# A hybrid decoder layer: the gated up projection as seven half-size products per pair of column tiles, with weight sums made by DMAs

## The chip, the cores and the metric

One core of a Trainium2 chip runs the whole layer. The time is device microseconds (us) of one execution; lower is better. The five engines are TensorE (PE, its weight loads shown apart as PEld), VectorE (DVE), ScalarE (ACT), GpSimd (POOL) and SyncE (SP, which only issues DMAs here).

## The reference, cut to what matters

The input x is 1024 tokens by 1024 channels in float32. The layer is a mixer (dilated attention heads beside mLSTM heads) and a gated ConvFFN, each with a residual; only the second is touched by the change.

```
def _conv_ffn(h, w_ffn_up, ffn_conv_w, ffn_conv_b, w_ffn_down):
    u = _causal_dwconv(h @ w_ffn_up, ffn_conv_w, ffn_conv_b)   # 1024 -> 2 x 2816, three taps over tokens
    gate, val = jnp.split(u, 2, axis=-1)
    return (jax.nn.silu(gate) * val) @ w_ffn_down               # 2816 -> 1024
...
h = h + _hybrid_mixer(_rmsnorm(h, mixer_norm_w[layer]), ...)
h = h + _conv_ffn(_rmsnorm(h, ffn_norm_w[layer]), ...)
return _rmsnorm(h, final_norm_w)
```

## The kernel before, in words

Every large product is computed from float32 operands split in two parts of a narrower format, a high part (a rounded copy) and a low part (the operand minus that copy). `mm3` issues three matmuls for one product: high by high, high by low, low by high. All matmuls of the up and down projections have a 128x128 stationary and a 512 wide moving operand and accumulate in one of eight PSUM banks (`bank`).

The kernel text is a planner. Each piece of work is a generator (a "lane") with a priority; `Clock` keeps an estimate of when each engine, tile and page is free, and `Lanes.run` takes the next lane that can go on. So the order of every engine's instructions is fixed when the program is built, and each engine runs its own list in order. SBUF tiles come from 48 pages of 128x1040 float32 (`page`, `free`); a lane waits until enough pages are free (`keep`). All plain loads and stores go through SP's queue in one order (`dma`, `store`).

The stages in order of time: input projection with mLSTM and attention (to about 530 us), output projection with the second norm (`output`, `h2`, to about 590 us), up projection (`upward`, to about 1070 us), down projection (`downward`, to the end).

- `h2` takes a finished residual tile `h` (128 tokens), normalises it into `xn2`, has PE transpose it in two groups of four, and writes the transposed tile as a high part `x2h` (ACT) and a low part `x2l` (DVE). The residual tiles `h` stay in SBUF to the end.
- `ufeed` loads the 44 column tiles of the up weights, 512 KB each, and splits them (`w..h`, `w..l`).
- `upward` walks the 44 column tiles (a gate tile, then the value tile of the same pair; 22 pairs). Each tile takes two token halves, and each half is 8 x 3 = 24 matmuls into one bank. `conv` then reads the bank: ACT writes the last tap into `ua`, DVE adds the other two taps, two small `edge` operations carry two tokens over the border of the halves; silu on the gate tile, and one product of both tiles. Gated tiles 0 to 7 stay in SBUF (`KEEP`), the other 14 are stored to DRAM (`gp`) and loaded again (`g`) for the down projection.
- `downward` already uses seven half-size products in place of eight (`seq`, `add_d`), with operands `A` (gated tiles) and `B` (down weights, loaded as `br`). Sums of quarters of the down weights are made in DRAM early on by `sums`: 4 copies issued by ACT and 7 adding DMAs issued by POOL, 2816 KB each, into `tsum`.

Two operations that can run on DVE or POOL are given to whichever the planner expects to finish first (`two`).

Of the kernel before, what the change touches and what calls it, by code (L numbers as in the profile page):

```python
# [15 lines left out]
S = 1024  # L16
D = 1024
# [206 lines left out]
def tile_hybrid_layer(ctx, tc, xT, x, w_t, w_v, w_g, w_o, w_up, w_dq, params, fnw, c_id, c_att, c_sel,  # L224
# [13 lines left out]
    tsum = {p: dram.tile([DFF // 2, 512], F32, name=f"tsum{p}") for p in (4, 5, 6, 7)}  # L238
    ctx.enter_context(tc.manual_schedule())
# [530 lines left out]
    def sums():  # L770

        quarter = lambda a, b: w_dq[a, b].rearrange("(r c) n -> r (c n)", c=4)
        into = {p: t.rearrange("(r c) n -> r (c n)", c=4) for p, t in tsum.items()}
        t = 100
        for p, b in ((5, (0, 0)), (6, (1, 1)), (7, (0, 1)), (4, (1, 0))):
            yield need(cond=lambda: clk.eng.get("pe", 0.0) > t)
            nc.scalar.dma_start(into[p], quarter(*b))
            t += 25
        for p, b in ((5, (0, 1)), (6, (0, 0)), (7, (1, 1)), (4, (1, 1)), (6, (0, 1)), (4, (0, 0)), (4, (0, 1))):
            yield need(cond=lambda: clk.eng.get("pe", 0.0) > t)  # L780
            nc.gpsimd.dma_start(into[p], quarter(*b), accum_op=OP.add, max_dma_last_dim=8192)
# [317 lines left out]
    ufeed = Feed([[w_up[c]] for c in range(2 * NK)], 2, 4, wait=lambda: "x2" in flags)  # L1099
    ufeed.start()  # L1100
# [17 lines left out]
    x2h, x2l = [], []  # L1118
# [13 lines left out]
    def output():  # L1132
# [52 lines left out]
    def h2(i, po):  # L1185
# [6 lines left out]
        for g in range(2):  # L1192
            yield need(xn_, bk=1)
            p = bank("ph2")
            for f in range(4):
                pe.transpose(p[:, f * 128:(f + 1) * 128], xn_[:, (g * 4 + f) * 128:(g * 4 + f + 1) * 128], ident)
            yield need(p)
            for f in range(4):
                ft = g * 4 + f
                wc = pr[:, P_FN + ft:P_FN + ft + 1]  # L1200
                ps_ = p[:, f * 128:(f + 1) * 128]
                act.activation(x2h[ft][:, ts], ps_, AF.Copy, scale=wc)
            yield need(x2h[g * 4 + 3])
# [11 lines left out]
        half_ready[i] = max(clk.ready(x2l[7]), clk.ready(x2l[3]))  # L1215
# [7 lines left out]
    KEEP = 8  # L1223
    LA = 5
    gate, gpage, gparked = {}, {}, set()
    gp = [dram.tile([128, 1024], F32, name=f"gp{k}") for k in range(NK)]

    def conv(c, ps):
        ch = (c // 2) + (c % 2) * NK
        cw = lambda j: pr[:, P_FW + ch * 3 + j:P_FW + ch * 3 + j + 1]  # L1230
        edge = small.tile([128, 2], F32, name="edge", bufs=4)
        for hf in range(2):
            yield need(pg=0 if hf else 1, cond=lambda: fin_ready(ps, hf))
            if hf == 0:
                a = page("ua")
            p = ps[hf]
            ah = a[:, H[hf]]
            act.activation(ah, p, AF.Identity, scale=cw(2), bias=pr[:, P_FB + ch:P_FB + ch + 1])
            yield need(a)
            for j in (1, 0):  # L1240
                sh = 2 - j
                dve.scalar_tensor_tensor(ah[:, sh:], p[:, :512 - sh], cw(j), ah[:, sh:], op0=OP.mult, op1=OP.add)
            if hf == 0:
                dve.tensor_scalar(edge, p[:, 510:512], cw(0), None, op0=OP.mult)
                dve.scalar_tensor_tensor(edge[:, 0:1], p[:, 511:512], cw(1), edge[:, 0:1], op0=OP.mult, op1=OP.add)
            else:
                dve.tensor_add(ah[:, 0:2], ah[:, 0:2], edge)
            freebank(p)
        yield need(a)
        if c % 2 == 0:  # L1250
            act.activation(a[:, :S], a[:, :S], AF.Silu)
            gate[c // 2] = a
        else:
            k = c // 2
            yield need(cond=lambda: k in gate)
            g = gate.pop(k)
            yield need(g)
            dve.tensor_mul(a[:, :S], a[:, :S], g[:, :S])
            free(g)
            if k < KEEP:  # L1260
                gpage[k] = a
            else:
                yield need(a)
                store(gp[k], a[:, :S])
                free(a)
                gparked.add(k)
# [56 lines left out]
    ADD, SUB = OP.add, OP.subtract  # L1323
# [7 lines left out]
    L, U = slice(0, 512), slice(512, 1024)  # L1331
# [9 lines left out]
    def split(t, src):  # L1341

        copy(t[:, L], src)
        yield need(t[:, L])
        two(t[:, U], src, f32(t[:, L]), OP.subtract)
# [75 lines left out]
    def add_d(j, p, to, done):  # L1421
        yield need(p)
        for th, hf, op in to:
            i = 4 * th + j
            dve.tensor_tensor(hp[i][:, H[hf]], hp[i][:, H[hf]], p, op=op)
# [5 lines left out]
        yield need(hp[i], pg=2)  # L1431
# [5 lines left out]
        act.activation(junk[:, h_], hp[i][:, h_], AF.Square, accum_out=(st2, st3)[hf][:, i:i + 1])  # L1437
        dve.tensor_mul(outs[i][:, h_], hp[i][:, h_], fins[0][:, h_])
# [18 lines left out]
    lanes.add(reload_gates(), 1)  # L1457
    lanes.add(b_load(), 1.1)
# [87 lines left out]
```

## Time and profile before

| | |
|---|---|
| median of 3 runs | 1291.52 us (1290.19 to 1293.23) |
| profiled execution | 1292.97 us |
| its span, first to last instruction | 1291.1 us |
| PE busy | 1277.5 us, 99% |
| DVE, ACT, POOL busy | 772.0, 502.8, 275.5 us |
| DMA traffic | 136.42 MB |

The page has busy time by engine, the span in 40 slices, the chain of work that ended last, and the costliest groups. All recorded instructions carry line 153, a helper that records every operation, so groups are told apart by their tiles (out <- in) and shapes. A matmul's row gives a duration longer than its share of the engine, since matmuls overlap; the pace is read from how many start in a stretch.

### The profile page before, as it was taken

What the parts mean: (1) busy time and instruction counts of PE and PEld (TensorE: products, weight loads), DVE (VectorE), ACT (ScalarE), POOL (GpSimd) and SP (SyncE); (2) the same over time, 40 slices, a digit from 0 to 9 for tenths busy, and PEclk for the clock granted to TensorE, in tenths of its full rate; (3) what the DMA queues carried; (4) which work ended last, traced back from release to release, by engine and by line L of the source; (5) the groups of instructions that cost most, each with busy time, mean ns of one, the idle gap of its engine ahead of it and who ended that gap; (6) DMA issues with size and microseconds to landing.
All of it is one profiled execution on the core that took longest, in us unless ns stands there. A gap on an engine that the chain in (4) does not pass through costs nothing.

```text
span 1291.1 us, 17082 instructions
## 1 busy us (share of the span) xinstructions
PE 1277.5 (99%) x6630; PEld 1079.7 (84%) x6630; DVE 772.0 (60%) x1511; ACT 502.8 (39%) x932; POOL 275.5 (21%) x162
## 2 busy tenths in 40 slices
PE   9999999999999989999999999999999999999997
PEld 6899898988998978888888888888888888888886
DVE  6726766678768786465343444434443556877865
ACT  4454354457656665153211121121212224243553
POOL 4420113022122022100222222222122110425002
PEclk9999999999999999999999999999999999999999
DMA  9404546651717552012111111313121217432324
GB/s 334 156 1 139 196 170 158 172 139 41 155 35 199 126 198 99 1 33 82 49 49 34 49 33 50 98 49 98 49 90 57 74 58 280 153 96 85 106 90 147
DMA packets 41001, 136.42 MB, mean 106 GB/s; under 512 B 4404, under 2 KB 5940, under 8 KB 38200
## 3 DMA queue, kind: packets, MB, share of 16 engines
q1 hardware_dynamic: 38024, 103.61, 23.5%
q0 software_dynamic: 2576, 20.19, 7.9%
q10 hardware_dynamic: 320, 11.53, 2.6%
q8 instruction: 52, 0.85, 0.3%
q14 instruction: 29, 0.24, 0.1%
HBM read 119.58 MB, written 47.45 MB: 129 GB/s over the span
## 4 chain that ended last, share of the span: by engine, by line
PE 95%; DVE 2%; ACT 1%; SPq 1%; issue 0%; DMA 0%; POOL 0%; POOLq 0%; DVEq 0%
PE bank L153 95%; DVE gu L153 1%; SPq L290 1%; DVE rows L153 0%; DMA xr<-in_xT_dram 0%; DVE q L153 0%; ACT L153 0%; DVE lf L153 0%; DVE ge L153 0%; ACT P L153 0%; ACT w1h L153 0%; ACT PT L153 0%; POOL w0l L153 0%; DVE gt L153 0%; DVE kS L153 0%
## 5 line engine op out<-in xcount | busy, mean ns | idle before, releaser
L153 DVE SCALAR_TENSOR_TENSOR ua<-bank,pr,ua 128x511 f32<-128x511 f32 (+1 forms) x176 | 131.9, 749 | 267.4 <-ACT ua L153 264.3
L153 PE MATMUL bank<-B,A 128*128 128x512 f32 x924 | 213.7, 393 | 0.0
L153 PEld LDWEIGHTS bank<-B,A 128*128 128x128 f32 x924 | 173.6, 188 | 40.0
L153 ACT ACTIVATE ua<-bank,pr 128x512 f32<-128x512 f32 x88 | 68.6, 779 | 341.0 <-PE bank L153 340.4
L153 DVE TENSOR_TENSOR h<-h,bank 128x512 f32<-128x512 f32 x88 | 56.9, 683 | 50.2 <-PE bank L153 50.2
L153 DVE CUSTOM_DVE_ANT_0 P<-bank,matt 128x512 f32<-128x512 f32 (+3 forms) x96 | 50.5, 551 | 14.9 <-PE bank L153 14.7
L153 ACT ACTIVATE P<-P,nmx 128x128 f32<-128x128 f32 (+3 forms) x64 | 49.4, 774 | 17.8 <-DVE nmx L153 16.8
L153 DVE TENSOR_TENSOR B<-br,B 128x512 fp32r<-128x512 f32 x67 | 49.7, 743 | 8.1 <-ACT B L153 7.9
L153 DVE TENSOR_TENSOR PT<-bank,PT 128x512 fp32r<-128x512 f32 (+1 forms) x80 | 47.7, 629 | 6.4 <-ACT PT L153 6.0
L153 PEld LDWEIGHTS bank<-PT,av 128*128 128x128 f32 x320 | 44.9, 192 | 3.8 <-DVE PT L153 1.5
L153 PE MATMUL bank<-PT,av 128*128 128x256 f32 (+1 forms) x320 | 46.9, 281 | 1.0 <-DVE PT L153 1.0
L153 ACT ACTIVATE B<-br 128x512 fp32r<-128x512 f32 x68 | 42.0, 620 | 6.1 <-DMA br<-in_w_dq_dram 4.1
L153 PE MATMUL bank<-kS,q 128*128 128x512 f32 (+3 forms) x192 | 41.9, 351 | 2.2 <-DVE OT L153 2.2
L153 ACT ACTIVATE PT<-bank 128x512 fp32r<-128x512 f32 (+1 forms) x72 | 37.4, 550 | 16.5 <-PE bank L153 15.0
L153 ACT ACTIVATE A<-g 128x512 fp32r<-128x512 f32 x45 | 28.0, 625 | 35.9 <-PE bank L153 15.9
L153 PE MATMUL bank<-ident,P 128*128 128x128 f32 x288 | 39.4, 274 | 0.2 <-ACT P L153 0.2
L153 ACT ACTIVATE A<-ua 128x512 fp32r<-128x512 f32 x31 | 19.4, 629 | 50.0 <-DVE ua L153 37.4
L153 ACT ACTIVATE ua<-ua 128x1024 f32<-128x1024 f32 x22 | 23.3, 1060 | 39.4 <-DVE ua L153 39.4
L153 PEld LDWEIGHTS bank<-kS,q 128*128 128x128 f32 x192 | 31.7, 192 | 6.1 <-issue 2.6
L153 POOL TENSOR_TENSOR rs<-st,half 128x1 f32<-128x1 f32 x16 | 12.1, 761 | 109.5 <-DVE st L153 109.5
L153 PEld LDWEIGHTS bank<-ident,P 128*128 128x128 f32 x288 | 32.4, 141 | 3.0 <-ACT P L153 1.2
L153 DVE SCALAR_TENSOR_TENSOR mqk<-mz,pr,mqk 128x1023 f32<-128x1023 f32 (+2 forms) x24 | 34.4, 1459 | 0.0
(674 smaller groups left out, 3579.6 us busy)
## 6 DMA issues: line engine op xcount, KB each, us to landing
wr<-in_w_up_dram SPq DMA_DIRECT2D x44, 512.0 KB, 3.8
tsum<-in_w_dq_dram POOLq DMA_DIRECT2D x7, 2816.0 KB, 17.5
tsum<-in_w_dq_dram ACTq DMA_DIRECT2D x4, 2816.0 KB, 11.4
br<-tsum SPq DMA_DIRECT2D x44, 256.0 KB, 2.7
br<-in_w_dq_dram SPq DMA_DIRECT2D x33, 256.0 KB, 2.7
gp<-ua SPq DMA_DIRECT2D x14, 512.0 KB, 2.9
g<-gp SPq DMA_DIRECT2D x14, 512.0 KB, 7.2
wr<-in_w_t_dram SPq DMA_DIRECT2D x13, 512.0 KB, 4.8
```

The lines of the kernel that those rows point to most:

```text
L153: r = f(*a, **k)
L290: nc.sync.dma_start(dst, src)
```

## The change

The up projection of a pair is now treated as a 2 by 2 block product: rows are the gate and the value tile, the inner dimension is cut in two halves of 512 channels, the columns are the two token halves. Seven products of half the inner length (4 x 3 = 12 matmuls each, numbered 1 to 7) take the place of eight.

- Input side: `h2` writes the transposed tiles unsplit into `x2f` (ACT alone). New lanes `x_block` make seven operand blocks `xb1` to `xb7` of four pages each (high part in the lower, low part in the upper half of a page): blocks 1, 2, 3 are parts of x2f, blocks 6, 5, 7, 4 are differences made in place by `two` (with four pages `xt`), each then split.
- Weight side: `usum` holds four summed quarters of the up weights in DRAM, made by `sums` with ACT copies and adding POOL DMAs of 5632 KB each, one after the other (5 from weights; 6 from 5; 3 from 6; 7 from weights). The sums for the down weights are now made the same way (4 copies, 4 adding DMAs) and later. `u_load` loads 256 KB per product into halves of a page `ur`; `u_side` splits it into `W`.
- Order of products: for the first four pairs 1 and 2 of each pair, then 3 of each, then 6, 5, 7, 4 pair by pair; for the other 18 pairs 1, 2, 6, 5, 3, 7, 4.
- `u_evac` combines the products with the sums in `ut`, partly in the bank itself, and `conv_half` does the taps for one half.
- All 22 gated tiles are stored and reloaded; the residual tiles are stored to `hpark` after `h2` and reloaded as `hq` in the down stage.

The core of the diff:

```
-            act.activation(x2h[ft][:, ts], ps_, AF.Copy, scale=wc)
-            dve.scalar_tensor_tensor(x2l[ft][:, ts], ps_, wc, f32(x2h[ft][:, ts]), op0=OP.mult, op1=OP.subtract)
+            act.activation(x2f[ft][:, ts], p[:, f * 128:(f + 1) * 128], AF.Copy, scale=wc)
+        store(hpark[i], hp[i][:, :S])
+        free(hp[i])
...
+    lanes.add(sums(70, 55, uq, usum, ((5, (1, 0), 0), (5, (1, 1), 1), (6, 5, 0), (6, (0, 0), 1), (3, 6, 0),
+                                      (3, (0, 1), 1), (7, (1, 0), 0), (7, (0, 0), 1))), 0.5)
+    lanes.add(sums(530, 45, dq, tsum, ((5, (0, 0), 0), (5, (0, 1), 1), (6, 5, 0), (6, (1, 1), 1), (4, 6, 0),
+                                       (4, (1, 0), 1), (7, (0, 1), 0), (7, (1, 1), 1))), 0.6)
...
+    usteps = [(c, p) for c in range(NP) for p in (1, 2)] + [(c, 3) for c in range(NP)]
+    usteps += [(c, p) for c in range(NP) for p in (6, 5, 7, 4)]
+    usteps += [(c, p) for c in range(NP, NK) for p in (1, 2, 6, 5, 3, 7, 4)]
...
-                    for k in range(8):
-                        mm3(p, wh[:, ks], wl[:, ks], x2h[k][:, sl], x2l[k][:, sl], k == 0, k == 7)
+            for f in range(4):
+                mm3(b, w[:, fs], w[:, fl], x_[:, L], x_[:, U], f == 0, f == 3)
+            lanes.add(u_evac(c, p, b), 3)
...
+        if p == 2:
+            dve.tensor_tensor(b, b, t[:, L], op=ADD)
+            yield from conv_half(c, 0, 0, b)
+        elif p == 6:
+            dve.tensor_tensor(t[:, L], t[:, L], b, op=SUB)
...
+        elif p == 7:
+            dve.tensor_tensor(t[:, L], t[:, L], b, op=ADD)
+            b = q5.pop(c)
+            dve.tensor_tensor(b, b, t[:, L], op=SUB)
+            yield from conv_half(c, 1, 1, b)
+        else:
+            dve.tensor_tensor(b, b, t[:, L], op=SUB)
+            yield from conv_half(c, 1, 0, b)
...
+    def reload_h():
+        for i in (0, 4, 1, 5, 2, 6, 3, 7):
+            yield need(pg=1, keep=8, cond=lambda: "up" in flags and used[0] > 2)
+            dma(hq[i][:, :S], hpark[i])
```

PE, where the up stage begins, before: x2h and x2l are the moving tiles of one channel block, w0h and w0l the split weights, and the transposes are of token tiles 6 and 7.

```order
L153 MATMUL bank3_86<-x2h0_5190,w0h_5216 128x512
L153 MATMUL bank3_86<-x2l0_5191,w0h_5216 128x512
L153 MATMUL bank3_86<-x2h0_5190,w0l_5217 128x512
L153 MATMUL bank6_89<-ident_92,xn2_5605 128x128 x4
L153 MATMUL bank3_86<-x2h1_5192,w0h_5216 128x512
L153 MATMUL bank3_86<-x2l1_5193,w0h_5216 128x512
```

So the three matmuls of one channel block follow each other, eight blocks to a bank.

PE, the same place now: product 1 of the first pair, with the transposes of tiles 5 and 6 inside it, and the first matmuls of product 2.

```order
L153 MATMUL bank1_96<-xb1_5465,W_5219 128x512 x3
L153 MATMUL bank2_97<-ident_104,xn2_5589 128x128 x4
L153 MATMUL bank3_98<-ident_104,xn2_5589 128x128 x4
L153 MATMUL bank6_101<-ident_104,xn2_5591 128x128 x4
L153 MATMUL bank4_99<-ident_104,xn2_5591 128x128 x4
L153 MATMUL bank1_96<-xb1_5468,W_5219 128x512 x3
L153 MATMUL bank1_96<-xb1_5470,W_5219 128x512 x3
L153 MATMUL bank1_96<-xb1_5472,W_5219 128x512 x3
L153 MATMUL bank0_95<-xb2_5474,W_5222 128x512 x3
```

A bank is now complete after 12 matmuls instead of 24, and three tiles' transposes stand inside the up stage instead of two.

DVE, from the last normed tile `xn2` on, before: the split of one weight tile, the taps of the first bank, and the low parts of the tile's transposes.

```order
L153 TENSOR_SCALAR xn2_5669<-h7_4998,rs2_109 128x1024
L153 CAST w3h_5679<-wr3_5613 128x1024
L153 TENSOR_TENSOR w3l_5680<-wr3_5613,w3h_5679 128x1024
L153 SCALAR_TENSOR_TENSOR ua_5677<-bank3_86,pr_91,ua_5677 128x511
L153 SCALAR_TENSOR_TENSOR ua_5677<-bank3_86,pr_91,ua_5677 128x510
L153 TENSOR_SCALAR edge_5622<-bank3_86,pr_91 128x2
L153 SCALAR_TENSOR_TENSOR edge_5622<-bank3_86,pr_91,edge_5622 128x1
L153 SCALAR_TENSOR_TENSOR x2l0_5191<-bank7_90,pr_91,x2h0_5190 128x128
```

Seven more x2l follow, and with them the operands of the whole up stage were complete.

DVE, the end of what stands there now, ahead of the first product 7: the last of blocks 7 and 4, a combination of product 6, and the low part of that product's weights (W_5979).

```order
L153 TENSOR_TENSOR W_5939<-ur_5793,W_5939 128x512
L153 TENSOR_TENSOR xb4_5909<-x2f5_5204,xb4_5909 128x512
L153 TENSOR_TENSOR xb7_5927<-xt_5731,xb7_5927 128x512
L153 TENSOR_TENSOR x2f6_5205<-x2f6_5205,xt_5731 128x512
L153 TENSOR_TENSOR xb7_5929<-xt_5732,xb7_5929 128x512
L153 TENSOR_TENSOR x2f7_5206<-x2f7_5206,xt_5732 128x512
L153 TENSOR_TENSOR ut_5645<-ut_5645,bank1_96 128x512
L153 TENSOR_TENSOR xb4_5946<-x2f6_5205,xb4_5946 128x512
L153 TENSOR_TENSOR W_5979<-ur_5976,W_5979 128x512
```

From the last `xn2` to W_5979 there are now 62 DVE instructions: 38 additions or subtractions of two SBUF tiles, 3 casts, 5 that take a bank, 8 taps and 8 edge operations.

ACT, in the input projection, before: a plain copy of a quarter of the down weights.

```order
L153 ACTIVATE va2_1577<-bank0_83,rn_101 128x128
L153 ACTIVATE va3_1579<-bank0_83,rn_101 128x128
L777 DMA tsum4_77<-in_w_dq_dram 64x11264
L153 ACT_TABLE_LOAD
L153 ACTIVATE mqk_1504<-mqk_1504 128x1024
```

Its source is an input, so ACT had nothing to wait for.

ACT, a few instructions further on in the same place now: a copy out of a sum that POOL's adding DMA has to have finished.

```order
L153 ACTIVATE mqk_1515<-mqk_1515 128x1024
L153 ACTIVATE va2_1588<-bank4_99,rn_113 128x128
L153 ACTIVATE va3_1590<-bank4_99,rn_113 128x128
L783 DMA usum6_83<-usum5_82 128x11264
L153 ACTIVATE va2_1588<-bank6_101,rn_113 128x128
```

Here ACT waits until that adding DMA has landed, with everything behind it on its queue. The adding DMA stands on POOL behind the split of w5 (`w5l`) and ahead of that of w6; two such waits of ACT lie in the input projection (usum6 from usum5, usum3 from usum6). Apart from the DMA issues that moved, the order of the engines before the second norm is as it was.

## Rows read from the trace of the kernel before

**Rows 1.** The page: busy time by engine, and the chain that ended last.
```profile
PE 1277.5 (99%) x6630; PEld 1079.7 (84%) x6630; DVE 772.0 (60%) x1511; ACT 502.8 (39%) x932; POOL 275.5 (21%) x162
PE 95%; DVE 2%; ACT 1%; SPq 1%; issue 0%; DMA 0%; POOL 0%; POOLq 0%; DVEq 0%
```
**Rows 2.** Stretches: us, busy PE (count) PEld DVE ACT POOL, PEclk, DMA share, GB/s.
```profile
579.80:1065.00 485.20, 485.20 (x2107) 393.86 (x2106) 215.06 (x397) 102.27 (x135) 96.84 (x41) 1.00 0.19 62
700.00:800.00 100.00, 100.00 (x434) 81.17 (x433) 41.09 (x77) 19.33 (x23) 21.66 (x9) 1.00 0.16 48
```
**Rows 3.** DVE, whole span, groups by shape: operation, count, busy us, mean ns, idle before.
```profile
L153 DVE SCALAR_TENSOR_TENSOR ua<-bank,pr,ua 128x511 f32<-128x511 f32 x88 | 66.0, 749 | 264.3 <-ACT ua L153 264.3
...
L153 DVE TENSOR_TENSOR h<-h,bank 128x512 f32<-128x512 f32 x88 | 56.9, 683 | 50.2 <-PE bank L153 50.2
...
L153 DVE TENSOR_TENSOR ua<-ua 128x1024 f32<-128x1024 f32 x22 | 27.0, 1225 | 0.7
...
L153 DVE TENSOR_TENSOR A<-g,A 128x512 fp32r<-128x512 f32 x37 | 25.5, 691 | 9.6 <-ACT A L153 9.5
...
L153 DVE SCALAR_TENSOR_TENSOR edge<-bank,pr,edge 128x1 f32<-128x1 f32 x44 | 9.6, 219 | 1.6
```
**Rows 4.** ACT, whole span, groups by shape.
```profile
L153 ACT ACTIVATE ua<-bank,pr 128x512 f32<-128x512 f32 x88 | 68.6, 779 | 341.0 <-PE bank L153 340.4 <-DVE B L153 0.6
L153 ACT ACTIVATE B<-br 128x512 fp32r<-128x512 f32 x68 | 42.0, 620 | 6.1 <-DMA br<-in_w_dq_dram 4.1 <-DVE B L153 1.3 <-POOL B L153 0.6
...
L153 ACT ACTIVATE ua<-ua 128x1024 f32<-128x1024 f32 x22 | 23.3, 1060 | 39.4 <-DVE ua L153 39.4
```
**Rows 5.** POOL from 1065 us on, groups by shape.
```profile
L153 POOL TENSOR_TENSOR B<-br,B 128x512 fp32r<-128x512 f32 x10 | 13.5, 1347 | 0.0
```
**Rows 6.** Timeline of PE in the second norm: start, us, engine, operation.
```profile
561.43 0.60 PE L153 MATMUL bank<-ident,xn 128*128 128x128 f32 x4
561.78 0.48 PE L153 MATMUL bank<-w2h,yh 128*128 128x512 f32 x1
```
**Rows 7.** Timeline of ACT, same stage.
```profile
581.32 1.14 ACT L153 ACTIVATE x2h<-bank,pr 128x128 fp32r<-128x128 f32 x4 [2.26 <-PE bank L153]
```
**Rows 8.** Timeline of DVE and POOL in the down projection.
```profile
1093.60 1.52 POOL L153 TENSOR_TENSOR ua<-ua,g 128x512 f32<-128x512 f32 x1 [50.80 <-DMA g<-gp]
1093.88 1.80 DVE L153 TENSOR_TENSOR ua<-ua,g 128x512 f32<-128x512 f32 x1
...
1099.11 9.66 DVE L153 TENSOR_TENSOR h<-h,bank 128x512 f32<-128x512 f32 x16 [1.38 <-PE bank L153]
...
1102.15 1.30 POOL L153 TENSOR_TENSOR A<-ua,A 128x512 fp32r<-128x512 f32 x1 [0.74 <-ACT A L153]
```
**Rows 9.** Stretches of 5 us around the one longer gap of PE, columns as in Rows 2.
```profile
455.00:460.00 5.00, 4.46 (x26) 3.46 (x25) 4.86 (x17) 3.55 (x7) 3.48 (x2) 1.00 1.02 416
...
465.00:470.00 5.00, 2.80 (x15) 2.02 (x14) 4.94 (x7) 3.00 (x5) 0.21 (x2) 1.00 0.05 20
470.00:475.00 5.00, 5.00 (x27) 4.76 (x26) 3.50 (x15) 1.70 (x7) 0.00 (x0) 0.66 0.38 108
```
**Rows 10.** DMA issues of the page: KB each, median us to landing.
```profile
wr<-in_w_up_dram SPq DMA_DIRECT2D x44, 512.0 KB, 3.8
...
tsum<-in_w_dq_dram ACTq DMA_DIRECT2D x4, 2816.0 KB, 11.4
...
g<-gp SPq DMA_DIRECT2D x14, 512.0 KB, 7.2
```
**Rows 11.** POOL's adding DMAs of 2816 KB (the line that issues them).
```profile
L781 POOL DMA_DIRECT2D tsum<-in_w_dq_dram x7: 920/982/1135, 197.6 to 415.7; - x7
...
DMA to landing us min/median/max: 17.1/17.5/20.5
```
**Rows 12.** Timeline of POOL in the input projection.
```profile
127.50 2.78 POOL L153 TENSOR_TENSOR w5l<-wr,w5h 128x1024 fp32r<-128x1024 f32 x1 [46.74 <-DVE ge L153]
```
**Rows 13.** Timeline of ACT in the input projection.
```profile
184.89 0.61 ACT L153 ACTIVATE va<-bank,rn 128x128 f32<-128x128 f32 x2
```

More of the change, by code (lines that the diff above doesn't have):

```diff
@@ L238, in tile_hybrid_layer @@
     tsum = {p: dram.tile([DFF // 2, 512], F32, name=f"tsum{p}") for p in (4, 5, 6, 7)}
+    usum = {p: dram.tile([DFF, 512], F32, name=f"usum{p}") for p in (3, 5, 6, 7)}
+    hpark = [dram.tile([128, 1024], F32, name=f"hpark{i}") for i in range(8)]
     ctx.enter_context(tc.manual_schedule())
@@ L1222, in tile_hybrid_layer @@
     NH = NK // 2
-    KEEP = 8
     LA = 5
+    LU = 5
+    NP = 4
     gate, gpage, gparked = {}, {}, set()
     gp = [dram.tile([128, 1024], F32, name=f"gp{k}") for k in range(NK)]
-    def conv(c, ps):
-        ch = (c // 2) + (c % 2) * NK
-        cw = lambda j: pr[:, P_FW + ch * 3 + j:P_FW + ch * 3 + j + 1]
[L1231 to L1245, printed above, removed]
-            else:
[L1247 to L1252, printed above, removed]
-        else:
[L1254 to L1266, printed above, removed]
@@ new lines, in tile_hybrid_layer, with two, split @@
+    L, U = slice(0, 512), slice(512, 1024)
+    ADD, SUB = OP.add, OP.subtract
+    def two(out_, a, b, op):
+        end = {}
+        for n in ("dve", "pool"):
+            c = clk.cost(n, "tensor_tensor", [out_], [a, b], {})
+            end[n] = clk.start(n, c, [out_], [a, b]) + c
+        (pool if end["pool"] + 0.3 < end["dve"] else dve).tensor_tensor(out_, a, b, op=op)
+    def split(t, src):
+        copy(t[:, L], src)
+        yield need(t[:, L])
+        two(t[:, U], src, f32(t[:, L]), SUB)
@@ new lines, in blocks_ready, with x_block @@
+    def blocks_ready(hf):
+        r = [half_ready.get(i, INF) for i in range(4 * hf, 4 * hf + 4)]
+        return max(r) if max(r) < INF else False
+    xb = {}
+    def x_block(p, f, src, wait, sums=(), done=()):
+        yield need(pg=1, keep=2, cond=wait)
+        t = page(f"xb{p}", F32R)
+        for s_ in sums:
+            two(*[s_[0](), s_[1](), s_[2]()], SUB)
+        yield need(src())
+        yield from split(t, src())
+        xb.setdefault(p, {})[f] = t
+        for d in done:
+            free(d())
@@ new lines, in u_side, with conv_half @@
+    def u_side():
+        for n in range(len(usteps)):
+            yield need(cond=lambda: n in uraw and n < uused[0] + LU)
+            r = uraw.pop(n)
+            src = r[:, (L, U)[n % 2]]
+            yield need(src, pg=1, keep=1 if xdone() else 2)
+            t = page("W", F32R)
+            yield from split(t, src)
+            if n % 2:
+                free(r)
+            Ub[n] = t
+    lanes.add(u_load(), 1.3)
+    lanes.add(u_side(), 2.5)
+    ut, ua, q5, edges = {}, {}, {}, {}
+    def conv_half(c, isv, hf, p, held=True):
+        ch = c + isv * NK
+        cw = lambda j: pr[:, P_FW + ch * 3 + j:P_FW + ch * 3 + j + 1]
+        if hf == 0:
+            yield need(pg=1)
+            ua[c, isv] = page("ua")
+            edges[c, isv] = small.tile([128, 2], F32, name="edge", bufs=8)
+        else:
+            yield need(cond=lambda: (c, isv, 0) in flags)
+        a, edge = ua[c, isv], edges[c, isv]
+        yield need(p)
+        ah = a[:, H[hf]]
+        act.activation(ah, p, AF.Identity, scale=cw(2), bias=pr[:, P_FB + ch:P_FB + ch + 1])
+        yield need(a)
+        for j in (1, 0):
+            sh = 2 - j
+            dve.scalar_tensor_tensor(ah[:, sh:], p[:, :512 - sh], cw(j), ah[:, sh:], op0=OP.mult, op1=OP.add)
+        if hf == 0:
+            dve.tensor_scalar(edge, p[:, 510:512], cw(0), None, op0=OP.mult)
+            dve.scalar_tensor_tensor(edge[:, 0:1], p[:, 511:512], cw(1), edge[:, 0:1], op0=OP.mult, op1=OP.add)
+        else:
+            dve.tensor_add(ah[:, 0:2], ah[:, 0:2], edge)
+        if held:
+            freebank(p)
+        flags.add((c, isv, hf))
+        if hf == 0:
+            return
+        del ua[c, isv], edges[c, isv]
+        yield need(a)
+        if not isv:
+            act.activation(a[:, :S], a[:, :S], AF.Silu)
+            gate[c] = a
+            return
+        yield need(cond=lambda: c in gate)
+        g = gate.pop(c)
+        yield need(g)
+        dve.tensor_mul(a[:, :S], a[:, :S], g[:, :S])
+        free(g)
+        yield need(a)
+        store(gp[c], a[:, :S])
+        free(a)
+        gparked.add(c)
@@ L1330, in tile_hybrid_layer @@
     used = [0]
-    L, U = slice(0, 512), slice(512, 1024)
-    def two(out_, a, b, op):
-        end = {}
-        for n in ("dve", "pool"):
-            c = clk.cost(n, "tensor_tensor", [out_], [a, b], {})
-            end[n] = clk.start(n, c, [out_], [a, b]) + c
-        (pool if end["pool"] + 0.3 < end["dve"] else dve).tensor_tensor(out_, a, b, op=op)
[L1341 to L1345, printed above, removed]
     def reload_gates():
-        for k in range(KEEP, NK):
-            yield need(pg=1, keep=6 if "up" in flags else 10, cond=lambda: "ending" in flags and k in gparked
+        for k in range(NK):
+            yield need(pg=1, keep=6, cond=lambda: "ending" in flags and k in gparked
                        and k < used[0] + 7)
@@ L1457, in tile_hybrid_layer @@
     lanes.add(reload_gates(), 1)
+    lanes.add(reload_h(), 1.05)
     lanes.add(b_load(), 1.1)
```

182 lines of the change are left out of this document (116 added, 66 removed).

## The prediction

> **What bounds the kernel now.** I read the busy times and the chain first. PE is busy for 1277.5 of 1291.1 us, and 95% of the chain that ended last is PE [rows 1]: the reader is to see that the time is the sum of PE's matmuls, and that only a removed matmul or a new PE gap moves the end. Then the stretches: through the whole up stage PE has no idle time at full granted clock, while DVE is busy 215.1, ACT 102.3 and POOL 96.8 of 485.2 us [rows 2]. There is room beside PE, most of it on ACT and POOL. The pace is 434 matmuls in 100 us, 0.2304 us each [rows 2].
>
> **What is removed.** A pair took 2 tiles x 2 halves x 24 = 96 matmuls and takes 7 x 12 = 84, of the same shape and with one weight load each as before. 22 x 12 = 264 fewer: 264 x 0.2304 = 60.8 us, all on PE's path. The order of PE bears that out: the whole program has 264 matmuls fewer, the transposes are as many as before.
>
> **What it adds in the steady part (pairs 5 to 22).** PE needs 84 x 0.2304 = 19.35 us per pair. The order of DVE now has per pair 8 taps, 7 combinations that read a bank, 3 splits and 1 cast of weights, 6 edge operations, 1 product of 1024; the other 4 splits are POOL's. From [rows 3], with 0.691 for the splits and the cast and 0.219 for every edge operation: 8 x 0.749 + 7 x 0.683 + 4 x 0.691 + 6 x 0.219 + 1.225 = 6.0 + 4.8 + 2.8 + 1.3 + 1.2 = 16.1 us. ACT, with each pair's copy of product 1 and six weight copies at 0.620: 4 x 0.779 + 7 x 0.620 + 1.060 = 8.5 us [rows 4]. POOL: 4 x 1.347 = 5.4 us [rows 5]. All are under 19.35, so I cost the steady part at nothing; its cover is 19.35 - 16.1 = 3.2 us of DVE per pair. Banks do not run out: a bank is held for one product (2.76 us) plus its evacuation; the longest, product 5, waits two more products for product 7 and then for two combinations, ACT and two taps, about 9.2 us; with seven a pair that is some 41 bank-us out of 8 x 19.35 = 155. The four adds that write back into a bank have no row; the nearest (bank in, SBUF out) is 0.683, which I take; the upper end is the 1.80 us of a blocked DVE add [rows 8], which would make 16.1 + 4 x 1.12 = 20.6 and cost 18 x 1.2 = 22 us.
>
> **POOL beside DVE.** In the down stage a DVE add of two SBUF tiles took 1.80 us instead of 0.691 while POOL worked, yet 16 adds that read a bank ran in 9.66 us, 0.604 each, with POOL busy beside them [rows 3, 8]. So only DVE work with two SBUF inputs suffers: 4 or 5 of some 26 instructions of a pair. At worst every POOL split delays DVE by its length, 5.4 us, and 16.1 + 5.4 = 21.5 us is 2.1 us over PE's pace. The Trainium skill, SBUF — State Buffer, "Who interferes with whom", states it as an exclusive lock between GpSimd and DVE instructions with two SBUF inputs or in a two-port mode; the trace agrees with it (1.80 against 0.604), and the rule speaks against this change, which puts more of exactly such work on both. By the lock at its worst the sum below would be 38 us worse; the order leaves DVE bank work to do meanwhile, so I leave it to a rival.
>
> **The head of the up stage.** This is where I expect a stall. Before, tile 7's transposes were the last thing missing. Now, between the last normed tile and the first product 7, DVE has 62 instructions: 38 on two SBUF tiles and 3 casts, 5 with a bank, 8 taps, 8 edge operations: 41 x 0.691 + 5 x 0.683 + 8 x 0.749 + 8 x 0.219 = 28.3 + 3.4 + 6.0 + 1.8 = 39.5 us [rows 3]. The means overlap by 0.08 us an instruction (0.683 against 0.604 back to back [rows 3, 8]), so 34.6 us is the lower end; add 1.9 us in which the third block waits for tile 7's transposes (0.9 us) and eight ACT copies (2.3 us, [rows 7]), less two instructions: 36.5 to 41.4. PE has in that time 8 transposes (two groups, each 0.32 + 0.09 = 0.44 us with the slower next matmul, [rows 6]) and 11 products and three quarters: 0.9 + 141 x 0.2304 = 33.4 us. PE waits 3.1 to 8.0 us, and up to 5 x 1.35 = 6.7 more if five POOL splits and sums block DVE [rows 5, 8]; I take the back-to-back pace, since DVE does not pause there, and half the block: 3.1 + 3.4 = 6.5, ends 3 and 15. A PE gap has a second price: after 2.2 us of idle PE the granted clock was 0.66 for 5 us, between the two levels of 1.2 and 2.4 GHz [rows 9], 1.7 us lost. Before that, two tiles' copies and a square now stand together on ACT ahead of tile 7: 1 us (0 to 3). Afterwards, in the 16 products of the first four pairs, DVE has about 48 us against 44 of PE, but the banks it frees are needed six or more products later; nothing. Head: 6.5 + 1.7 + 1 = 9.2 us.
>
> **The moved DMAs.** The copy of twice the bytes should take 2 x 11.4 = 22.8 us and the adding one 35 to 41 us [rows 10, 11]. It is issued when POOL is done with w5l, at 130.3 us [rows 12], and lands by 171; ACT asks for it behind 185.5 us [rows 13]. 14 us to spare, the second such wait has more. Price 0 (0 to 5). The stores of `h` and of eight more gated tiles wait on SP for work already done; behind each store stand loads needed ten products (27.6 us) later: 0.
>
> **Up to down.** Eight more gated tiles and eight residual tiles, 8 MB, are loaded around the boundary, and the last two of product 1's operands stand behind the residuals on SP's queue. These 4.2 MB, asked for three steps into the down stage, take 10 us at the 416 GB/s that a full stretch reached [rows 9] and 14 at 300; the step that needs what is behind them comes 16.6 us later, with 2 us of splitting between. I take 1.5 us, 0 to 5 (a gated tile took 7.2 us to land when many were asked for, [rows 10]).
>
> **The sum.** 60.8 - 9.2 - 1.5 = 50.1 us. The profiled execution took 1292.97 us (span 1291.1), so 1242.9; it lies 1.45 us over the median of 1291.52, so 1241.4 in its terms, rounded 1241.
>
> **The rivals.**
> 1. *No stall at the head*: POOL takes its share without blocking and DVE keeps back-to-back pace: 60.8 less at most 2 us, 1231 to 1233. Against it: 33.4 us of PE under 36.5 us of DVE.
> 2. *The lock bounds the steady part*: 18 x 2.1 = 38 us on top, 1279; with half the blocks DVE is at 18.8 us, under PE's pace, and nothing is lost. For it 1.80 us [rows 8]; against it the few instructions that can collide.
> 3. *DMAs*: an adding DMA at half the pace (70 to 82 us) holds ACT for 15 to 27 us behind 185.5 us, and PE for most of it, since ACT empties the banks there; or the boundary costs 10: 1250 to 1265. Against: [rows 11] show 20.5 us at most for seven of them beside weight loads.
> 4. *Slower than before*: the adds that write into the bank they read. If each took 2.4 us, DVE would have 16.1 + 4 x 1.7 = 22.9 us a pair, 3.5 over PE, 22 x 3.5 = 78 us lost and 1319. It decides from 2.2 us per add (then 51 us are lost, all that the sum left). No row shows such an add; the nearest is 0.683 [rows 3].
>
> That PE does not get the matmuls back is excluded by its order.
>
> **How the numbers follow.** Forecast (PE bound, one stall at the head, 1234 to 1250) 0.72; rival 1 0.10; rival 2 0.06; rival 3 0.08; rival 4 0.04. The range takes in the forecast's ends (a head stall of 3 to 15 us, 0 to 5 at each of two places), rival 1 and most of rival 3: 1231 to 1260. A difference of 0.2% is about what a measurement of this kernel can tell from no change. Faster 0.95, same 0.01, slower 0.04.
>
> **What would show it.** Right: PE busy near 1218 us; one PE gap of 3 to 15 us around 620 us, released by DVE's xb7, xb4 or W; afterwards 19.3 to 19.5 us per pair; DVE near 16 us of each; no ACT wait for usum. Wrong: PE gaps in every pair (rivals 2 and 4; the duration of `bank<-bank,ut` and of `W` on DVE tells them apart), an ACT wait before its copy of usum near 185 us, or a gap at the first steps of the down stage.

## The result, and the profile after

| | before | after |
|---|---|---|
| median | 1290.9 us (1290.19 to 1293.23, 4 runs) | 1234.83 us (1232.74 to 1236.24, 4 runs) |
| profiled execution, its span | 1292.97, 1291.1 us | 1236.24, 1234.4 us |
| PE busy | 1277.5 us | 1216.6 us |
| DVE, ACT, POOL busy | 772.0, 502.8, 275.5 us | 899.7, 590.3, 300.2 us |
| DMA traffic | 136.42 MB | 208.01 MB |

The ratio of after to before is 0.9561 (95% interval 0.9543 to 0.958): faster by 56 us. PE's busy time and the chain, on the page of after, answer to [rows 1]:

```profile
PE 1216.6 (99%) x6366; PEld 1027.3 (83%) x6366; DVE 899.7 (73%) x1692; ACT 590.3 (48%) x1108; POOL 300.2 (24%) x214
PE 93%; DVE 3%; issue 2%; ACT 1%; POOL 1%; DMA 0%; SPq 0%; POOLq 0%; DVEq 0%
```

PE has 264 instructions and 60.9 us of busy time less, and is still the bound. The stretches of after (us, busy PE with its count, PEclk, DMA share, GB/s) say where it is not busy inside and behind the up stage:

```profile
580.00:600.00 20.00, 19.89 (x91) 1.00 0.87 211
600.00:640.00 40.00, 36.31 (x147) 0.96 0.50 165
640.00:700.00 60.00, 60.00 (x261) 1.00 0.59 171
700.00:1000.00 300.00, 300.00 (x1297) 1.00 0.54 175
1000.00:1100.00 100.00, 100.00 (x435) 1.00 0.64 232
```

One place only, at 600 to 640 us. The timeline of PE there (start, us, operation, and in brackets the wait before it):

```profile
585.22 1.09 PE L153 MATMUL bank<-ident,xn 128*128 128x128 f32 x8
586.07 27.39 PE L153 MATMUL bank<-xb,W 128*128 128x512 f32 x117
613.63 0.73 PE L153 MATMUL bank<-xb,W 128*128 128x512 f32 x2 [0.17 <-ACT W L153]
616.40 5.57 PE L153 MATMUL bank<-xb,W 128*128 128x512 f32 x22 [2.04 <-POOL W L153]
622.36 0.74 PE L153 MATMUL bank<-xb,W 128*128 128x512 f32 x2 [0.39 <-ACT W L153]
624.18 16.18 PE L153 MATMUL bank<-xb,W 128*128 128x512 f32 x62 [1.08 <-DVE W L153]
```

Four stops, 3.7 us together, all for weights: the 2.04 is the weight of the first product 6, the 1.08 that of the first product 7 (W_5979). Behind them the granted clock was lower for one stretch of 5 us, as behind the old gap in [rows 9] (not in every execution: see e8):

```profile
625.00:630.00 5.00, 5.00 (x16) 0.66 0.84 313
```

What made PE wait is in the timelines of POOL and of DVE, and, behind them, of ACT and of SP:

```profile
609.18 1.29 POOL L153 TENSOR_TENSOR xb<-xt,xb 128x512 fp32r<-128x512 f32 x1 [18.24 <-ACT xb L153]
610.43 1.30 POOL L153 TENSOR_TENSOR x2f<-x2f,xt 128x512 f32<-128x512 f32 x1
611.68 1.30 POOL L153 TENSOR_TENSOR xb<-xt,xb 128x512 fp32r<-128x512 f32 x1
612.94 1.73 POOL L153 TENSOR_TENSOR x2f<-x2f,xt 128x512 f32<-128x512 f32 x1
614.63 1.71 POOL L153 TENSOR_TENSOR W<-ur,W 128x512 fp32r<-128x512 f32 x1
```

```profile
612.42 1.10 DVE L153 TENSOR_TENSOR xb<-x2f,xb 128x512 fp32r<-128x512 f32 x1 [0.45 <-ACT xb L153]
613.45 3.44 DVE L153 TENSOR_TENSOR xt<-xt,x2f 128x512 f32<-128x512 f32 x2
...
623.44 0.69 DVE L153 TENSOR_TENSOR W<-ur,W 128x512 fp32r<-128x512 f32 x1
```

```profile
612.96 0.62 ACT L153 ACTIVATE W<-ur 128x512 fp32r<-128x512 f32 x1
```

```profile
SPq L292 <- ACT xb L153: 29.2, 1, 29.2
SPq L292 <- POOL x2f L153: 5.1, 1, 5.1
```

The weight that PE wanted at 614.4 was the fifth in a row on POOL. While POOL ran, two DVE subtractions took 3.44 us; without POOL beside them two such take 1.28 (below, in e4). The last row of DVE is the low part of W_5979.

The queues are not all of it. The load of the first product 6's weight had landed at 597.5 us, but ACT's copy of it, which comes before POOL's part, ran at 612.96. The load of W_5979's weight was issued only at 614.7 us, after SP had stood for 34.3 us (29.2 and 5.1) before pages that other tiles held. Until the last block stands, `u_load` goes on only with eight free pages and `u_side` only with three, and block 4 is what frees the pages of `x2f` and `xt`. So a shortage of pages sets, beside the queues, how late these weights are; no run changes the number of pages by itself.

The steady part, 680 to 980 us, 15.5 pairs: two of DVE's groups by shape (count, busy us, mean ns, idle before), and the stretch as a whole (busy PE, PEld, DVE, ACT, POOL):

```profile
L153 DVE TENSOR_TENSOR bank<-bank,ut 128x512 f32<-128x512 f32 x62 | 43.2, 697 | 31.4 <-PE bank L153 30.5
L153 DVE TENSOR_TENSOR W<-ur,W 128x512 fp32r<-128x512 f32 x47 | 32.3, 687 | 8.7 <-ACT W L153 8.1
```

```profile
680.00:980.00 300.00, 300.00 (x1297) 243.21 (x1296) 227.92 (x406) 120.99 (x187) 79.85 (x64) 1.00 0.53 168
```

An add that writes back into its bank takes 0.697 us, little more than the 0.687 of a split. In these 300 us PE is never idle, and DVE is busy for 227.9 us, 14.7 per pair.

### The profile page after: what moved, and what is told of

Read it like the earlier page. It is cut to its first block, busy times and chain, and to the rows that moved or that the text cites. A ratio compares the mean times of both kernels' runs of the same rounds, so it can differ in the third digit from the quotient of the medians.

```text
span 1234.4 us, 17447 instructions
## 1 busy us (share of the span) xinstructions
PE 1216.6 (99%) x6366; PEld 1027.3 (83%) x6366; DVE 899.7 (73%) x1692; ACT 590.3 (48%) x1108; POOL 300.2 (24%) x214
## 2 busy tenths in 40 slices
DMA packets 63805, 208.01 MB, mean 169 GB/s; under 512 B 6756, under 2 KB 8292, under 8 KB 58728
## 3 DMA queue, kind: packets, MB, share of 16 engines
q1 hardware_dynamic: 58472, 137.69, 31.5%
## 4 chain that ended last, share of the span: by engine, by line
PE 93%; DVE 3%; issue 2%; ACT 1%; POOL 1%; DMA 0%; SPq 0%; POOLq 0%; DVEq 0%
PE bank L153 93%; DVE gu L153 1%; DVE rows L153 0%; POOL w0l L153 0%; DVE xt L153 0%; DMA w0r<-in_w_t_dram 0%; DVE q L153 0%; ACT L153 0%; SPq L292 0%; DVE xb L153 0%; POOL rs L153 0%; DVE lf L153 0%; DVE ge L153 0%; ACT P L153 0%; ACT w1h L153 0%
## 5 line engine op out<-in xcount | busy, mean ns | idle before, releaser
L153 PE MATMUL bank<-xb,W 128*128 128x512 f32 x1848 | 431.6, 395 | 3.7 <-POOL W L153 2.0
L153 PEld LDWEIGHTS bank<-xb,W 128*128 128x128 f32 x1848 | 347.6, 188 | 86.6 <-POOL W L153 2.5
L153 PEld LDWEIGHTS bank<-B,A 128*128 128x128 f32 x924 | 173.6, 188 | 39.7
L153 POOL TENSOR_TENSOR W<-ur,W 128x512 fp32r<-128x512 f32 x83 | 107.3, 1311 | 282.0 <-ACT W L153 272.2
L153 DVE SCALAR_TENSOR_TENSOR ua<-bank,pr,ua 128x511 f32<-128x511 f32 (+1 forms) x168 | 125.3, 746 | 15.9 <-ACT ua L153 12.9
L153 ACT ACTIVATE W<-ur 128x512 fp32r<-128x512 f32 x133 | 78.3, 623 | 18.6 <-DMA ur<-usum 18.0
L153 DVE TENSOR_TENSOR bank<-bank,ut 128x512 f32<-128x512 f32 x84 | 58.5, 696 | 34.1 <-PE bank L153 33.0
L153 DVE CUSTOM_DVE_ANT_0 P<-bank,matt 128x512 f32<-128x512 f32 (+3 forms) x96 | 50.5, 551 | 14.9 <-PE bank L153 14.7
L153 DVE TENSOR_TENSOR ut<-ut,bank 128x512 f32<-128x512 f32 x66 | 44.9, 681 | 19.4 <-PE bank L153 19.0
L153 DVE TENSOR_TENSOR W<-ur,W 128x512 fp32r<-128x512 f32 x71 | 49.4, 701 | 8.8 <-ACT W L153 8.1
L153 POOL TENSOR_TENSOR A<-g,A 128x512 fp32r<-128x512 f32 x17 | 23.2, 1370 | 121.8 <-ACT A L153 121.7
L153 DVE TENSOR_TENSOR A<-g,A 128x512 fp32r<-128x512 f32 x60 | 41.7, 699 | 14.2 <-ACT A L153 13.8
L153 ACT ACTIVATE B<-br 128x512 fp32r<-128x512 f32 x69 | 42.3, 619 | 16.1 <-DMA br<-in_w_dq_dram 10.5
L153 DVE TENSOR_TENSOR hq<-hq,bank 128x512 f32<-128x512 f32 x56 | 34.9, 679 | 20.5 <-PE bank L153 20.5
## 6 DMA issues: line engine op xcount, KB each, us to landing
usum<-in_w_uq_dram POOLq DMA_DIRECT2D x4, 5632.0 KB, 34.4
usum<-in_w_uq_dram ACTq DMA_DIRECT2D x2, 5632.0 KB, 20.9
usum<-usum ACTq DMA_DIRECT2D x2, 5632.0 KB, 22.1
```

Of the source, the lines that this page charges most:

```text
L153: r = f(*a, **k)
```

## The experiments

Medians; the kernel before, measured beside them, was at 1290.4 to 1291.3 us, and after is 1234.8. The theory: the time is PE's matmuls, plus one stall at the head of the up stage, made by the queue of block and weight work on DVE and POOL; everything else lies under PE.

| | edit | us | ratio to before, 95% |
|---|---|---|---|
| e1 | one product more per pair | 1293.7 | 1.0014 to 1.0033 |
| e2 | before, with parking alone | 1294.4 | 1.0018 to 1.0038 |
| e3 | no block sums | 1230.2 | 0.952 to 0.9546 |
| e4 | POOL off the head | 1239.4 | 0.9591 to 0.9617 |
| e5 | two pairs at the head | 1249.1 | 0.9663 to 0.9689 |
| e6 | six pairs at the head | 1241.9 | 0.9604 to 0.9631 |
| e7 | 4 more DVE adds per pair | 1234.1 | 0.9547 to 0.9573 |
| e8 | 8 more DVE adds per pair | 1243.2 | 0.9611 to 0.9646 |
| e9 | weights 9 ahead | 1230.9 | 0.9524 to 0.9551 |
| e10 | weights 11 ahead | 1232.3 | 0.9536 to 0.9562 |
| e11 | weight sums 22 us apart | 1253.3 | 0.9699 to 0.9726 |

**e1, the matmuls given back.**

```
-            for f in range(4):
+            for f in (*range(4), *range(4)) if p == 2 else range(4):
```

> The changed kernel with one product more per pair: each pair's second product is computed twice into the same bank, 12 x 22 = 264 matmuls given back, all other work unchanged. Theory (the gain is the matmuls, and a stall of 3.7 us with 1.6 us of lower clock at the head of the up stage is all that was lost): 264 x 0.2304 = +60.8 us; the four doubled products at the head are 11 us of more cover, so the stall and the clock's loss go: 1234.8 + 60.8 - 3.7 to - 5.3 = 1290 to 1292, the time of the kernel before. Rival (the other work that the change adds costs PE something outside the head, paid for by something else that the change saves): another sum, below 1287 or above 1295.

```profile
PE 1276.0 (99%) x6630; PEld 1076.8 (83%) x6630; DVE 902.8 (70%) x1688; ACT 593.5 (46%) x1112; POOL 298.9 (23%) x214
```

1293.7, between the two: 58.9 us over after in the medians. In the traces PE's busy time is 1276.0 and 1216.6, 59.4 apart. The spans are 1290.7 and 1234.4, 56.3 apart: the 60.8 less the stops that went (3.7 to 1.1, one wait left) and the 1.8 us of longer busy time (lower clock and interrupted runs) that e3 measures. So the matmuls are the gain. The medians are 2.6 us further apart than the spans because the profiled execution of after lies 1.4 us over its median and that of e1 1.2 under; why e1's median lies over the range of the theory is not explained.

**e2, parking alone.** The kernel before with `KEEP = 0` and `h` stored after `h2` and read back as `hq`.

> The kernel before, with the residual tiles and all gated tiles parked in DRAM and read back as in the changed kernel, and nothing else of the change. Theory (parking lies beside other work on every queue): the time of the kernel before within 0.2%, 1289 to 1294. Rival (the 16 more tiles that go out and come back delay the down stage's first pages, and the change's gain hides it): 1295 or more, with PE idle at the change from up to down.

1294.4: about 4 us slower, just over the theory's range and short of the rival. In its trace 1.7 us of that is a PE wait that the kernel before does not have, in the first steps of the down stage:

```profile
PE bank L153 <- POOL A L153: 1.7, 1, 1.7
```

After has no PE wait in that stretch, so in it parking is covered; in the old order it is not quite. The other 2 us were not located.

**e3, without the block sums.**

```
-        for s_ in sums:
-            two(*[s_[0](), s_[1](), s_[2]()], SUB)
```

Products 6 and 7 then take plain blocks (two more lines, not shown), so the kernel leaves that part of the computation out.

> The changed kernel without the 16 subtractions that form the activation blocks of products 6, 7 and 4: those products take plain blocks instead (that part of the computation is left out), with the same splits and matmuls. Theory (the head's wait is the queue of block building on DVE and POOL): 16 x 0.69 = 11 us of work fewer ahead of the first product 4, so the 3.7 us stall goes and with it most of the 1.6 us of lower clock: 1229.5 to 1231.5. Rival (the stall is the weights' splits or their loads, not the blocks): within 1 us of the changed kernel's 1234.8.

1230.2. PE has no wait in the head (600 to 640 us: 40.00 of 40, clock 1.00), and PE's busy time is 1214.8, 1.8 less than after. So the head's loss is 3.7 + 1.8 = 5.5 us in the traces (5.7 by the spans; 4.7 by the medians, since the profiled execution of after is its slowest), and it goes with the block sums. But two things went together: with the blocks done sooner, pages came free sooner, and the load of the first product 7's weight was issued at 594.5 us instead of 614.7. This run does not say which of the two counts.

**e4, POOL off the head.**

```
         e = pool if end["pool"] + 0.3 < end["dve"] else dve
+        if not xfin:
+            e = dve
```

> The changed kernel with POOL kept off the activation blocks and the weight splits until the last activation block stands; DVE does them. Theory (POOL's slow subtractions, 1.5 to 1.7 us each, and the DVE work that stands still beside them cost more than the sharing saves): no wait for POOL's weights, 1231 to 1233. Rival (sharing pays): the six or so POOL instructions of that stretch are 6 x 0.69 = 4 us more in DVE's queue, all of it in the wait for the first products 5, 7 and 4: 1236 to 1239. Between the two, 1234 to 1235.5, what the lock takes and what sharing gives are alike.

1239.4: the rival, and a little more. The timelines of PE, of ACT ahead of the weight that PE waits for, and of DVE:

```profile
623.21 17.12 PE L153 MATMUL bank<-xb,W 128*128 128x512 f32 x59 [6.00 <-ACT W L153]
```

```profile
622.01 0.63 ACT L153 ACTIVATE xb<-x2f 128x512 fp32r<-128x512 f32 x1 [2.98 <-DVE x2f L153]
622.55 0.61 ACT L153 ACTIVATE W<-ur 128x512 fp32r<-128x512 f32 x1
```

```profile
612.86 1.28 DVE L153 TENSOR_TENSOR xt<-xt,x2f 128x512 f32<-128x512 f32 x2
```

The weight, landed at 599.0 us, has its copy on ACT behind a block's copy, and that waits for DVE's subtraction. DVE is now never held up (two `xt` in 1.28 us), but has all the work. So the mutual blocking costs DVE about 2.6 us in after, and sharing with POOL is worth 4.6 us more than it costs. The Trainium skill, Perfetto Trace Analysis, "Optimizing Scalar/DVE Operations", warns that moving work between GpSimd and DVE might not help, since they share a read port; here it does, by these 4.6 us, because POOL takes whole instructions off a queue on which PE waits.

**e5 and e6, two and six pairs at the head.** `NP = 2` and `NP = 6` instead of 4.

> The changed kernel with two pairs instead of four at the head for which the products 1, 2 and 3 come before all others (each such pair is 3 x 12 x 0.2304 = 8.3 us of matmuls ahead of the first product that needs a sum block). Theory (the head's wait is the block queue on DVE and POOL against what PE has to do meanwhile): 16.6 us of cover fewer, while DVE has the adds, filters and weight splits of two pairs' products (5 to 6 us each) fewer ahead of the last block; the stall grows by 16.6 - 11 = 5 to 6 us, with some more at the lower clock: 1239 to 1246. Rival (the stall is a queue order of POOL's own, not cover): 1234 to 1236.

> The changed kernel with six pairs instead of four at the head for which the products 1, 2 and 3 come first. Theory: 16.6 us of cover more against some 11 us of DVE work more, so a margin of 5 to 6 us more than the 3.7 us stall: the stall and its clock loss go, 1229.5 to 1231.5. Rival (POOL's queue order makes the stall, or more pairs in flight run out of pages and PE waits for a weight or a bank): 1234 or more.

With two pairs 1249.1, worse than expected. All PE waits in the head are now for blocks (line waited for: us, times, longest), and the clock falls to the lower of its two levels in the stretch that follows:

```profile
PE bank L153 <- DVE xb L153: 11.8, 4, 4.7
PE bank L153 <- ACT xb L153: 0.6, 1, 0.6
```

```profile
620.00:625.00 5.00, 4.22 (x10) 0.50 0.00 0
```

12.4 us of waits against 3.7, and PE's busy time 1221.3 against 1216.6: 8.7 + 4.7 = 13.4 us, where the spans are 12.4 and the medians 14.3 apart. A pair's cover is worth 4.3 us of waits, not the 2.8 I had put; that a pair has less DVE work ahead of the blocks than I counted would explain it, but is not shown.

With six pairs 1241.9: here the theory as I had put it falls, more cover made it slower. The PE waits of e6 from 575 to 680 us, SP's longest up to 626 us, and two rows of ACT:

```profile
PE bank L153 <- ACT W L153: 3.3, 2, 1.7
PE bank L153 <- POOL W L153: 2.6, 1, 2.6
PE bank L153 <- DVE W L153: 0.7, 1, 0.7
```

```profile
SPq L292 <- DVE xb L153: 25.5, 1, 25.5
SPq L292 <- POOL xt L153: 11.1, 1, 11.1
```

```profile
623.17 0.60 ACT L153 ACTIVATE ut<-bank 128x512 f32<-128x512 f32 x1 [5.29 <-PE bank L153]
...
624.19 0.62 ACT L153 ACTIVATE W<-ur 128x512 fp32r<-128x512 f32 x1
```

As in after, PE waits for weights alone, 6.6 us against 3.7. SP stood for most of 579.8 to 625.8 us before pages that other tiles still held, 36.6 us of it in the two waits shown, against 34.3 in after. But the loads are not what PE waited for: the two weights that came too late, those of the first two products 3, had landed at 597.5 and 598.2 us. Their copies on ACT ran at 614.5 and 624.2, the second behind the copy of a bank that PE itself had still to fill. `u_side` also asks for free pages before it splits a weight, and six pairs in work hold more of them; that this is what put the splits so late is argued from the kernel's text, and no run tests it. So with two pairs the blocks are the limit, with four and six the weights, which pages and queues delay together.

**e7 and e8, more DVE work in every steady pair.**

```
+            if c >= NP:
+                for _ in range(1):          # e8: 2
+                    dve.tensor_tensor(spare[:, L], b, t[:, L], op=ADD)
```

at four places of `u_evac`.

> The changed kernel with four more DVE instructions per pair from the fifth pair on, each an add of a bank and a tile into a spare tile (0.70 us, by the 0.697 of such an add), 2.8 us a pair. Theory (DVE's 14.7 us of each pair's 19.35 are cover): 17.5 us a pair, no change, 1233 to 1237. Rival (banks and weights come later because of DVE's queue, so its latency and not its throughput bounds the pairs): 1240 or more.

> The changed kernel with eight more such DVE instructions per pair, 5.6 us a pair. Theory: 14.7 + 5.6 = 20.3 us a pair, 0.95 over PE's 19.35, times 18 pairs = 17 us: about 1252 (1240 to 1262, since the planner moves weight splits to POOL, which takes work off DVE and stops it in turn). Rival (DVE has more room than its busy time says): within 3 us of the changed kernel.

e7: no change, as expected. e8 is 8.3 us slower, half of what I expected, and not where I expected it. Its steady stretch (PE, PEld, DVE, ACT, POOL), and then its PE waits from 980 to 1120 us:

```profile
680.00:980.00 300.00, 300.00 (x1297) 243.24 (x1296) 272.92 (x462) 123.83 (x199) 146.55 (x111) 1.00 0.55 171
```

```profile
PE bank L153 <- DVE ua L153: 3.0, 1, 3.0
PE bank L153 <- DVE A L153: 1.0, 1, 1.0
PE bank L153 <- ACT A L153: 0.7, 1, 0.7
```

DVE rose by 45 us only, since the planner gave POOL 109 splits instead of 62; PE did not stop once in the steady part, beside 146.6 us of POOL work. 4.7 us of waits are at the end of the up stage, where the delayed filters meet the down stage's operands; PE's busy time is 4.1 us longer too (1220.7), with a clock of 0.97 from 980 to 1100 us. The head of e8 adds something on the clock:

```profile
600.00:640.00 40.00, 36.31 (x153) 1.00 0.48 164
```

It has the same four stops as after, 3.7 us together, yet the clock stayed at 1.00. So the second price of the stops, 0.66 for 5 us in after, is not paid each time.

**e9 and e10, weights further ahead.** `LU = 9` and `LU = 11` instead of 5.

> The changed kernel with the up stage's weights loaded and split nine products ahead of PE instead of five (one number). Theory (the head's wait is the amount of work that stands on DVE and POOL between the normalised residual and the first product 7, weight splits among it): splits move ahead of that stretch, where DVE has idle time, and SP asks for pages earlier; two to four splits of 0.69 us and the waits for weights behind POOL go, and with the 3.7 us stall the 1.8 us of lower clock: 1229.5 to 1232. Rival (the pages that the weights hold are then missing for blocks and product tiles, as with six pairs): 1236 or more. Rival (the stall is the blocks' own length, whatever the weights do): 1234 to 1235.5.

> The same with eleven products ahead. Theory: as with nine, 1229.5 to 1232, nothing left to gain. Rival (pages): slower than with nine, 1234 or more.

e9: 1230.9, 4.0 us better than after; no PE wait in the head at all. DVE's last `xn2`, first copy of the third block and, in e9, the low part of the first product 7's weight; then the first two in after:

```profile
581.59 0.78 DVE L153 TENSOR_SCALAR xn<-h,rs 128x1024 f32<-128x1024 f32 x1
...
585.64 0.42 DVE L153 CAST xb<-x2f 128x512 fp32r<-128x512 f32 x1
...
617.00 1.29 DVE L153 TENSOR_TENSOR W<-ur,W 128x512 fp32r<-128x512 f32 x2
```

```profile
584.41 0.75 DVE L153 TENSOR_SCALAR xn<-h,rs 128x1024 f32<-128x1024 f32 x1 [0.69 <-POOL rs L153]
...
587.35 0.43 DVE L153 CAST xb<-x2f 128x512 fp32r<-128x512 f32 x1 [0.97 <-ACT x2f L153]
```

The whole block queue starts 1.7 us earlier, and up to 584 us DVE has done 22.8 us of work since 540 instead of 21.2. The first of the two weights at 617.00 is done at 617.7, where W_5979 was done at 624.1 in after: 6.4 us, of which 1.7 is the earlier start. The other 4.7 is a shorter queue, 53 DVE instructions from that copy on instead of 60, with three weight splits among them instead of seven. The block sums are all still there; so the head's loss goes without taking them out: with these weights early enough, they are covered. e10 is no better (the intervals overlap). SP stood for pages in both (31.5 and 33.3 us in its longest waits), but the weights needed first had been loaded before.

**e11, the weight sums closer together.** `sums(70, 22, ...)` instead of `sums(70, 55, ...)`.

> The changed kernel with the eight DMAs of the up weights' sums 22 us apart instead of 55, so that the copies that read a sum back (two of them, on ACT's queue) are issued 44 us after the copy and 22 us after the adding DMA on which they wait, which takes 34 us. Theory of the price (the margin of 14 us in the change's spacing is what keeps ACT free): ACT stands still 12 to 20 us twice between 90 and 200 us of the span, PE waits for what ACT was to do: 10 to 35 us slower than the changed kernel, 1245 to 1270. Rival (ACT's wait is covered by what PE has queued, or the engine doesn't stand still for it): within 3 us of 1234.8.

1253.3, 18.4 us slower. ACT in the input projection, and what PE then waited for:

```profile
180.09 0.48 ACTq L783 DMA_DIRECT2D usum<-usum  x1
180.66 1.06 ACT L153 ACTIVATE w7h<-wr 128x1024 fp32r<-128x1024 f32 x1 [16.80 <-DMA usum<-in_w_uq_dram]
```

```profile
184.78 0.80 PE L153 MATMUL bank<-mC,mqk 128*128 128x129 f32 x2 [15.14 <-DVE mC L153]
```

ACT stood with its queue behind a copy that waited for POOL's adding DMA, DVE stood for ACT (16.3 us, for `sc`), and PE's next operand was behind that. The other such wait, ahead of 124.4 us, was shorter (7.6 us without an ACT instruction), and no stop of PE is seen to follow from it: the next, 0.5 us for `rows`, is in after too (0.6), and one of 0.8 us for `mC` at 153 us was not traced back. From 100 to 200 us PE is busy for 83.6 us, in after for 99.4: 15.8 us, which is about the 15.7 between the spans; the medians are 18.4 apart. So rival 3's mechanism is real, and the spacing in the change is what keeps it away.

## Why the prediction was right

- **PE bounds, 60.8 us removed.** Measured 60.9 in PE's busy time, and e1 gives it back. Right. That it agrees to 0.1 us is luck: the 1216.6 of after holds 1.8 us of the head's loss, and the 1277.5 of before is 1.9 us over that of e2, which has as many matmuls (1275.6).
- **Steady part at nothing.** Right: no PE idle time from 640 to 1100 us. I had 16.1 us of DVE per pair, it is 14.7: I had added means, and instructions overlap, as the head's paragraph itself allowed for. Added that way, the groups measured in after make 15.9 a pair. The cover is 4.7 us, and e7 and e8 show that the planner's choice between DVE and POOL adds to it.
- **POOL beside DVE.** The rule of the Trainium skill (SBUF — State Buffer, "Who interferes with whom") shows in the head: 3.44 us against 1.28 for two subtractions, and POOL's own 1.73 against 1.29. It does not bound: e8 has POOL busy for 146.6 of 300 us without a PE stop. By the rule at its worst (rival 2, 38 us) the kernel would have been at 1279.
- **The head, 9.2 us.** Right in place and path, too large: 5.5. The last stop ends with DVE's W_5979, and DVE did not pause from 612.4 us on, so all stops together are the length of DVE's queue less PE's work. Not foreseen: there are four stops and not one gap, the longest (2.0 us) for a weight in POOL's queue, and the shortage of pages is in no term. DVE's queue from the last `xn2` to W_5979 ran 39.7 us (584.41 to 624.13), where 36.5 and a block of 2.6 (1.10 and 3.44 against 0.69 and 1.28) make 39.1; I had 3.4 for the block. The mis-sized term is PE's cover: 33.4 by count, but PE was at work for 624.18 - 584.41 - 3.7 = 36.1 us. 145 matmuls began in that time and not 141 (0.9 us), and each of four interrupted runs ends with 0.27 us beyond its pace (a run of two takes 0.73 us, two at pace 0.46), 1.1 us; 0.7 is not located. For the clock I had 1.7; e3 measures 1.8 for it and those ends together, and e8 shows that the clock's part does not always come. The 1 us for ACT ahead of tile 7 was 0.1. (In the transposes' term 0.32 should read 0.35, by [rows 6]; its sum of 0.44 is right.)
- **Moved DMAs, 0.** Right. The adding DMA took 34.4 us (I had 35 to 41), the copy 20.9 to 22.1 (22.8); ACT asked at 182.0, some 20 us after the landing at 162.2. e11 shows the price when it is not so.
- **Up to down, 1.5.** It was 0 here; e2 shows a wait of 1.7 there in the old order.
- **The sum.** 60.8 - 5.5 = 55.3, against 56.7 between the profiled executions and 56.1 between the medians. The predicted 1241 was 6 us high: 3.7 of it the head (9.2 - 5.5), 1.5 the boundary, the last microsecond not located. Rival 1 gives e9's time, 1231: it needed a change of one number.
- **Rival 4**: 0.697 us for the add into its bank settles it. Its price was reckoned with 22 pairs where the steady part has 18: 63 us, not 78.

## What to carry to other kernels

Removing matmuls from a PE that is busy all the time gives their time back at pace, as long as the added vector work stays under it; the cost is where the new operands are first made, and there the queue of the slower engines is to be counted against PE's work, each queue for itself, together with the pages that the work in it holds. The lookahead of weights and the number of products ahead of the first new operand are worth trying there; more is not always better: two, four and six pairs gave 1249, 1235 and 1242 us, five, nine and eleven weights 1235, 1231 and 1232. A copy that waits for an adding DMA belongs on a queue where nothing urgent is behind it, or well behind the landing.

## What the runs showed of the hardware

- A few short stops can cost PE more than their length. After 12.4 us of waits in e5 the granted clock was 0.50 in a stretch of 5 us, and PE's busy time 4.7 us longer than in after (ends of interrupted runs included). After 3.7 us in after it was 0.66 in one such stretch; after the same four stops in e8 it stayed at 1.00.
- DVE and POOL slowed each other by unlike amounts: two DVE subtractions went from 1.28 to 3.44 us, POOL's from 1.29 to 1.73.
- An adding DMA of 5632 KB took 34.4 us where a plain copy of the same size took 20.9 to 22.1.
